# An encoder block in float32: output projection and second MLP product turned to tokens on partitions

## The chip, the cores and the metric

The kernel runs on one core of one Trainium2 chip. The metric is device microseconds from start to end of one execution, the median over runs. TensorE multiplies a stationary 128x128 operand with a moving one of up to 512 columns and writes PSUM, which has eight banks of [128, 512] float32. DVE, ScalarE (ACT in the profile) and GpSimd (POOL) do the elementwise work, and nearly all DMAs are issued by SyncE (SP). Each engine takes its instructions in the order in which the program lists them.

## The reference

One layer of an encoder block over x of [512 tokens, 2048 features], in float32. What matters here is its end:

```python
mix = (gate_a * y_a + gate_b * y_b) @ w_o[l] + b_o[l]
x = layer_norm(DEEPNORM_ALPHA * x + g1 * mix, ln1_g[l], ln1_b[l])
h = x * (1.0 + sc2) + sh2
f = jnp.square(jax.nn.relu(h @ w_m1[l] + b_m1[l])) @ w_m2[l] + b_m2[l]
x = layer_norm(DEEPNORM_ALPHA * x + g2 * f, ln2_g[l], ln2_b[l])
```

`w_o` is [2048, 2048], `w_m1` [2048, 8192], `w_m2` [8192, 2048]. Both norms go over the 2048 features of a token. `g1`, `sc2`, `sh2` and `g2` are vectors over the features, products of the conditioning vector with `w_ada`.

## The kernel before

**Products.** Each float32 operand is split into a high part of float32r's width and a low part (`split`, lines 74 to 77: a cast on ScalarE, a subtraction on DVE), and each product is three: high by high, high by low, low by high. Weights come in blocks of 256 rows and 512 columns (512 KB). `Weights` (lines 112 to 152) keeps three raw blocks in flight and three split ones ready. `take` hands out a block and, just before, splits the next and asks SP for the load of another, into the raw buffer that this split sets free.

**Where the work lies.** From the branches on, activations have features on partitions and tokens along the free side. `dense` (lines 157 to 205) makes four products of 128 output features by 512 tokens, or by half of the tokens (`tok`): weights are stationary, activations move. After each block of weights it runs the steps listed in `stages` for that block. These lists are written by hand, and they set the order of all other work on every engine.

**Projection and first norm (lines 960 to 978).** Column groups 0 and 1 of `w_o` are made for all tokens, groups 2 and 3 for the first half of the tokens and then for the second, so that the first half's norm runs beside the second half's products; their weights are loaded twice. `add_to` (line 905) empties four banks with one DVE step each (gate, line 902) and adds to the sums of the norm: squares on ScalarE, sums on POOL (line 826) and DVE (line 827). `Norm` (lines 799 to 872) works across partitions: it shifts by the first group's mean (lines 804 to 814), adds up over partitions with products of one column (line 848), and spreads the result over the partitions with other products (line 863).

**The MLP (lines 1013 to 1029)** goes in eight slabs of 1024 hidden features: two groups of `w1` (`hidden`, line 981), then four of `w2` in `add_to`. The first slab makes its `w1` groups by halves of the tokens, beside the late half's norm and input (`second_input`, line 930), and `skip_path` (line 993) scales the residual on POOL. All blocks of `w1` of that slab come twice.

**The last slab (lines 1031 to 1055)** makes `w2` groups 2 and 3 by halves; their split blocks stay in 16 tiles (`wkeep`), since they are used twice. The late half's last group is emptied bank by bank (`add_late`, line 910). Behind the last product come the sums, the root, their spreading and eighteen steps of `normal_2` (line 998) on DVE, POOL and ScalarE, with the output's DMAs.

Of the kernel before, what the change touches and what calls it, by code (L numbers as in the profile page):

```python
# [40 lines left out]
def block_kernel(ctx: ExitStack, tc: tile.TileContext, t):  # L41
# [38 lines left out]
    def blocks():  # L80
# [5 lines left out]
        def groups():  # L86
# [25 lines left out]
    class Weights:  # L112
        """Blocks of 256 rows and 512 columns: loaded three ahead of their split, split ahead of their use."""
# [15 lines left out]
        def tiles(self, what):  # L129
            """For the parts of a block; those of the last ones stay."""  # L130
            if what[0] == t["w_m2"].name and what[1] >= NSLAB * 4 - 2:
# [3 lines left out]
            return [wts.tile([P, 1024], F32R, name=n, tag=n) for n in ("whi", "wlo")]  # L135

        def prepare(self):
            while self.raw and len(self.ready) <= self.ahead:
# [6 lines left out]
        def take(self, w, cg, kp):  # L145
            if (w.name, cg, kp) in self.used:
                return self.kept[w.name, cg, kp]
            self.prepare()
# [8 lines left out]
    def dense_steps(out, w, cg, pairs, act, tok=ALL, by_token=False, stages=None, tail=None):  # L157
        """Four products of 512 columns of w: [features, tokens], or by_token [tokens, features].
        A step takes 256 rows; the last two, with tail, bank by bank, and tail follows each."""
# [3 lines left out]

        def products(i, kp, hi, lo):
            for j in range(2):
# [3 lines left out]
                if by_token:  # L169
                    s = slice(i * P, (i + 1) * P)  # L170
                    c = slice(512 * j, 512 * (j + 1))
                    terms = (ah[:, s], hi[:, c]), (ah[:, s], lo[:, c]), (al[:, s], hi[:, c])
                else:
                    s = slice(512 * j + i * P, 512 * j + (i + 1) * P)
                    terms = (hi[:, s], ah[:, tok]), (hi[:, s], al[:, tok]), (lo[:, s], ah[:, tok])
                for m, (a, b) in enumerate(terms):
                    nc.tensor.matmul(out[i], a, b, start=first and m == 0, stop=last and m == 2)  # L177
                if not tail or kp < pairs - 2:
                    yield

        kept = []
        for kp in range(pairs):
            hi, lo = weights.take(w, cg, kp)
            if tail and kp >= pairs - 2:
                kept.append((kp, hi, lo))
                if len(kept) == 2:
                    for i in range(4):
                        for k_ in kept:
                            for _ in products(i, *k_):
                                pass  # L190
                        tail(i, out[i])
            else:
                live = [products(i, kp, hi, lo) for i in range(4)]
                for _ in range(2):
                    for g in live:
                        next(g)
# [12 lines left out]
    def rstd_of(var):  # L209
        """[P, n] variances -> 1 / sqrt(max(var, 0) + eps), with a Newton step behind the table's root."""  # L210
# [27 lines left out]
    mean4 = const.tile([P, P], F32, name="mean4")  # L238
    nc.vector.memset(mean4, 1.0 / 512.0)

# [33 lines left out]
    spec = dram.tile([2, 2, 4, 2, P, 512], F32, name="spec")  # L274

# [3 lines left out]
    class Sine:  # L279
        """sin(freq * (product + bias)), its argument brought into the table's range."""  # L280
# [17 lines left out]
    def table(name, tiles):  # L298
        """cosines of the classes 0, 2, 1, 3, their sines, and -sines and -cosines of class 3."""
# [6 lines left out]
    class Forward:  # L306
        """Transform of four [128 tokens of a class, 512 channels] (classes 0..3), for angles below pi / 4
        and by symmetry the rest. Sums over the even positions, then with those over the odd."""
# [4 lines left out]
        def minus(self, out, a, b):  # L313
            """a - b of cosines; b - a of sines."""
# [13 lines left out]
        def odd(self):  # L328
            """Both sums over the odd positions, where the other kind's aren't wanted."""
# [15 lines left out]
    #: The spectra's parts: order, half of the channels, cosine or sine.  # L345
    PARTS = [(o, hf, cs) for o, hf in ((1, 1), (1, 0), (0, 0), (0, 1)) for cs in range(2)]

    class Filters:
        """The spectra: they go to DRAM but for the first to be used."""
# [15 lines left out]
        def fetch(self, n):  # L365
            """Last layer's weights and, in the row below, the skip's; with a half's first, its window."""
# [12 lines left out]
        def mixed(self, n):  # L379
            """Weights of the even and the odd parts of the taps."""  # L380
# [42 lines left out]
    def first_input(kc, xt):  # L423
        """x's chunk, modulated, in two parts."""
# [8 lines left out]
    def short_conv(ps, which, hf):  # L433
        """[128 channels, 512 tokens] x 4."""
# [93 lines left out]
    def to_tokens(src, cl, dst):  # L528
        """Four [128 channels, 512 tokens] -> [128 tokens of a class, 512 channels]."""
# [7 lines left out]
    class Conv:  # L537
        """A long convolution of four [128 tokens of a class, 512 channels], in stages."""
# [4 lines left out]
        def odd(self):  # L543
            """Sums over the classes 1 and 3, of cosines and sines, for both kinds of angles."""
# [35 lines left out]
        def fold(self, part):  # L580
            """Frequencies -> inputs of the inverse, by class of tokens, in three steps."""
# [21 lines left out]
    #: The column of a class in the tables.  # L603
# [11 lines left out]
    def inverse_T(conv, i, gate):  # L615
        """The same, [128 channels, 512 tokens], and its product's parts."""
# [18 lines left out]
    def into(conv, src):  # L635
        """Stages that lead from channels to the conv's two transforms."""
# [5 lines left out]
    def between(conv):  # L642
        """The same, in the next group."""
# [3 lines left out]
    def out_of(conv, gate, dst, after):  # L647
        """Stages that lead from a conv to the next one's first transform."""
# [147 lines left out]
    class Norm:  # L796
        """Sums of the deviations of [P, 512] chunks from the first group's mean, and of their squares."""

        def __init__(self):
# [348 lines left out]
```

## Time and profile before

| | us |
|---|---|
| median of 3 runs | 2803.61 (2803.1 to 2805.07) |
| profiled execution, its span from first to last instruction | 2800.5 |
| median less span: what lies around it | 3.1 |
| TensorE busy (97% of the span) | 2723.1 |
| DVE busy (54%) | 1509.0 |
| ScalarE busy (30%) | 830.8 |
| POOL busy (10%) | 274.6 |
| first product of `w_o` starts | 1157.60 |
| first product of `w2`, first slab, starts | 1445.17 |
| first product of `w2`, last slab, starts | 2663.76 |
| last product of `w2` ends, about | 2772.0 |

The profile is of one execution; it gives the span of that execution, and no other time of its own, so the 3.1 us compare it with the median. The starts in the lower part cut the span into stages. A busy TensorE is not one at its peak: products overlap, and their ends are modelled, so the pace is read from the distance between starts.

### The profile page before, as it was taken

To read this page: it belongs to the slowest core of one execution; us is meant where nothing else is said; L and a number is where in the kernel's file an instruction comes from. 1 tells how busy PE (TensorE), PEld (TensorE's weight loads), DVE (VectorE), ACT (ScalarE), POOL (GpSimd) and SP (SyncE) were. 2 spreads that over 40 slices of the span, in tenths; PEclk is the share of its full clock that TensorE was granted. 3 is DMA by queue.
4 is the path that set the end of the run, shared out by engine and by line. 5 is a ranking of instruction groups with operands and counts; after the bars stand their busy time and mean duration, and the time that the engine had idled before them with its cause. 6 is when DMAs were issued, how large, how long until landed. Compare 5 with 4: busy or idle time off the path is not lost.

```text
span 2800.5 us, 31575 instructions
## 1 busy us (share of the span) xinstructions
PE 2723.1 (97%) x12680; PEld 2243.0 (80%) x12680; DVE 1509.0 (54%) x1958; ACT 830.8 (30%) x1034; POOL 274.6 (10%) x222
## 2 busy tenths in 40 slices
PE   6899999999999999999999999999999999999986
PEld 2487777888888888889998888888888888888876
DVE  8976978554565556458863233433333334333276
ACT  3334223222223222434641222312222122221234
POOL 6510000000000000013740000000000000000034
PEclk9899999999999999999999999999999999999998
DMA  9673332555565567335553333332333333233322
GB/s 310 229 279 113 121 105 98 195 195 195 197 210 188 196 216 265 115 127 173 177 155 98 98 98 98 98 95 95 97 98 98 98 98 98 91 99 97 98 78 74
DMA packets 120020, 396.40 MB, mean 142 GB/s; under 512 B 13979, under 2 KB 18075, under 8 KB 119872
## 3 DMA queue, kind: packets, MB, share of 16 engines
q1 hardware_dynamic: 119872, 394.37, 43.0%
q8 instruction: 99, 1.62, 0.2%
q14 instruction: 49, 0.40, 0.0%
HBM read 383.84 MB, written 10.49 MB: 141 GB/s over the span
## 4 chain that ended last, share of the span: by engine, by line
PE 90%; DVE 5%; POOL 2%; issue 1%; DMA 1%; ACT 1%; SPq 0%; DVEq 0%; POOLq 0%; ACTq 0%
PE d L177 85%; DVE araw L264 1%; PE flt L393 1%; DVE xr L869 1%; POOL h L937 1%; DVE wlo L77 1%; DMA araw<-in_ada 1%; PE inv L621 1%; PE inv L609 0%; DVE ln_s L827 0%; PE f_o L334 0%; PE f_ee L322 0%; PE f_eo L326 0%; PE tr L532 0%; PE mix L743 0%
## 5 line engine op out<-in xcount | busy, mean ns | idle before, releaser
L177 PE MATMUL d<-act,whi 128*128 128x512 f32 (+1 forms) x5120 | 1456.7, 370 | 4.9 <-DVE bf_e L318 1.5
L77 DVE TENSOR_TENSOR wlo<-wraw,whi 128x1024 fp32r<-128x1024 f32 x488 | 602.2, 1237 | 1080.4 <-ACT whi L76 1077.2
L177 PEld LDWEIGHTS d<-act,whi 128*128 128x128 f32 x5120 | 927.5, 189 | 173.0 <-issue 7.7
L76 ACT CAST whi<-wraw 128x1024 fp32r<-128x1024 f32 x488 | 512.4, 1053 | 1498.3 <-PE d L177 1462.5
L177 PE MATMUL d<-act,wlo 128*128 128x512 f32 (+1 forms) x2560 | 943.4, 369 | 9.9 <-DVE wlo L77 9.9
L177 PEld LDWEIGHTS d<-act,wlo 128*128 128x128 f32 x2560 | 483.0, 189 | 92.2 <-DVE wlo L77 11.7
L177 PE MATMUL d<-fh,whi 128*128 128x512 f32 x960 | 373.9, 389 | 0.0
L177 PE MATMUL d<-fh,wlo 128*128 128x512 f32 x960 | 373.5, 389 | 0.0
L177 PE MATMUL d<-fl,whi 128*128 128x512 f32 x960 | 373.5, 389 | 0.0
L264 DVE SCALAR_TENSOR_TENSOR araw<-araw,cond 128x1024 f32<-128x1024 f32 x192 | 255.1, 1349 | 7.0 <-DMA araw<-in_ada 6.8
L824 POOL COPY ln_s<-xr 128x512 f32<-128x512 f32 x2 | 1.9, 936 | 2272.1 <-DVE xr L814 2272.1
L177 PEld LDWEIGHTS d<-fl,whi 128*128 128x128 f32 x960 | 180.2, 188 | 37.6 <-issue 0.2
L177 PEld LDWEIGHTS d<-fh,whi 128*128 128x128 f32 x960 | 180.2, 188 | 37.6 <-issue 0.2
L177 PEld LDWEIGHTS d<-fh,wlo 128*128 128x128 f32 x960 | 180.2, 188 | 37.4
L902 DVE SCALAR_TENSOR_TENSOR xr<-d,mod,xr 128x512 f32<-128x512 f32 (+1 forms) x160 | 102.6, 695 | 47.4 <-PE d L177 47.4
L177 PE MATMUL d<-whi,act 128*128 128x512 f32 x256 | 78.9, 389 | 0.0
L990 DVE TENSOR_TENSOR relu<-relu 128x512 f32<-128x512 f32 (+1 forms) x72 | 46.1, 640 | 38.5 <-ACT fh L989 38.4
L397 POOL TENSOR_TENSOR flt<-flt,win 128x512 f32<-128x512 f32 x32 | 62.8, 1987 | 5.2 <-ACT flt L395 4.8
L177 PE MATMUL d<-fh,wkeep 128*128 128x256 f32 x256 | 51.3, 300 | 10.0 <-DVE wkeep L77 10.0
L988 ACT ACTIVATE relu<-d,c_bm 128x512 f32<-128x512 f32 (+1 forms) x72 | 45.3, 629 | 38.5 <-PE d L177 38.5
L177 PEld LDWEIGHTS d<-whi,act 128*128 128x128 f32 x256 | 48.0, 188 | 9.9
L872 POOL TENSOR_TENSOR xr<-xr,ln_m 128x256 f32<-128x256 f32 x54 | 48.1, 902 | 54.0 <-DVE xr L869 54.0
(212 smaller groups left out, 1951.4 us busy)
## 6 DMA issues: line engine op xcount, KB each, us to landing
wraw<-in_w_m SPq DMA_DIRECT2D x272, 512.0 KB, 3.5
araw<-in_ada SPq DMA_DIRECT2D x192, 512.0 KB, 4.6
wraw<-in_w_in SPq DMA_DIRECT2D x144, 512.0 KB, 3.5
wraw<-in_w_o SPq DMA_DIRECT2D x48, 512.0 KB, 3.7
spec<-spec SPq DMA_DIRECT2D x48, 256.0 KB, 5.0
wraw<-in_w_b SPq DMA_DIRECT2D x16, 512.0 KB, 3.5
wraw<-in_w_a SPq DMA_DIRECT2D x16, 512.0 KB, 3.4
xT<-in_xT SPq DMA_DIRECT2D x16, 256.0 KB, 5.8
```

Source lines behind the costliest of these rows:

```text
L76: nc.scalar.copy(hi, src)
L77: nc.vector.tensor_tensor(lo, src, f32(hi), op=OP.subtract)
L177: nc.tensor.matmul(out[i], a, b, start=first and m == 0, stop=last and m == 2)
L264: nc.vector.scalar_tensor_tensor(raw, raw, 1.0, cond[:, 1024 * h:1024 * (h + 1)], op0=OP.mult, op1=OP.mult, accum_out=dots[:, m, kc, h:h + 1])
L393: nc.tensor.matmul(ps, self.a2[:k, cl, :], w[:k], start=True, stop=True)
L397: nc.gpsimd.tensor_tensor(x, x, win, op=OP.mult)
L621: nc.tensor.matmul(ps[:, cl * P:(cl + 1) * P], conv.y[cl][cs][:, s], ic(4 * cs + COLUMN[cl]), start=(cs == 0), stop=(cs == 1))
L869: nc.vector.tensor_tensor(x, x, self.rs[:, tok], op=OP.mult)
L872: eng.tensor_tensor(x, x, self.mr[:, tok], op=OP.add)
L902: nc.vector.scalar_tensor_tensor(x, ps, gate_[:, n:n + 1], x, op0=OP.mult, op1=OP.add)
L988: nc.scalar.activation(r, ps[i], AF.Relu, bias=bm1[:, n:n + 1], scale=1.0)
L990: nc.vector.tensor_tensor(r, r, r, op=OP.mult)
```

## The change

The output projection and the second MLP product are made with activations stationary and weights moving (`token_dense`), so that their results have 128 tokens on partitions and 512 features along the free side. The residual is loaded in that layout (a new input `x`, beside the transposed one), and the output leaves in it. Vectors over the features become rows, broadcast over the partitions: the two gates through a transpose, a store to DRAM and loads back (`gate_rows`), the others from a new input `rows`. Both norms take their moments with `bn_stats` along the free side; the class `Norm` is gone. The MLP's input goes back to features on partitions with transposes on TensorE (`turned`). In the first slab one group of `w1` is made by halves and the other for all tokens. In the last slab, column groups 2 and 3 are made for one tile of 128 tokens after the other, and each tile's norm and output follow it. `prepare` splits at most four blocks at a time and no longer counts the kept ones.

The diff, cut to its core (comments that go away, and functions that are only removed, are left out):

```diff
-                for cg in range(n) if s else (0, 1, 0, 1):
+                for cg in range(n) if s else (0, 0, 1):
...
         def prepare(self):
-            while self.raw and len(self.ready) <= self.ahead:
+            for _ in range(4):
+                if not self.raw:
+                    return
+                ring = sum(not self.keeps(r[2]) for r in self.ready)
+                if ring > self.ahead and not self.keeps(self.raw[0][1]):
+                    return
                 raw, what = self.raw.pop(0)
...
+    def gate_rows():
+        both = small.tile([P, 2, KC], F32, name="gcols", tag="gcols")
+        nc.scalar.copy(both[:, 0], mod[:, 2])
+        nc.scalar.copy(both[:, 1], mod[:, 5])
+        ps = bank("gT")
+        nc.tensor.transpose(ps[:2 * KC, :P], both.rearrange("p g k -> p (g k)"), ident)
+        rows_ = slot("gT")
+        nc.scalar.copy(rows_[:2 * KC, :P], ps[:2 * KC, :P])
+        for i in range(2):
+            nc.sync.dma_start(grow[i].rearrange("(k p) -> k p", p=P), rows_[i * KC:(i + 1) * KC, :P])
+    def row(src, name="row"):
+        return load(slot(name), src.broadcast_to([P, 512]))
+    gate_rows()
+    g1_row = [wts.tile([P, 1024], F32, name="g1row", tag="araw") for _ in range(2)]
+    for i, g in enumerate(g1_row):
+        load(g, grow[0:1, 1024 * i:1024 * (i + 1)].broadcast_to([P, 1024]))
+    load(cond, grow[1:2].broadcast_to([P, D]))
...
+    def residual(c):
+        gb = row(t["rows"][0:1, COLS[c]])
+        nc.gpsimd.tensor_scalar(gb, gb, 1.0 / ALPHA, None, op0=OP.mult)
+        nc.gpsimd.tensor_tensor(gb, gb, g1_row[c], op=OP.mult)
+        for i in TILES:
+            r[i][c] = load(slot("r"), t["x"][i][:, COLS[c]])
+            nc.gpsimd.tensor_tensor(r[i][c], r[i][c], gb, op=OP.add)
+    def token_dense(w, cg, pairs, act, tiles=TILES, stages=None):
+        out = {i: bank("t") for i in tiles}
+        for kp in range(pairs):
+            hi, lo = weights.take(w, cg, kp)
+            for j in range(2):
+                kc = 2 * kp + j
+                ah, al = act[kc]
+                c = slice(512 * j, 512 * (j + 1))
+                for i in tiles:
+                    s = slice(i * P, (i + 1) * P)
+                    for m, (a, b) in enumerate(((ah[:, s], hi[:, c]), (ah[:, s], lo[:, c]), (al[:, s], hi[:, c]))):
+                        nc.tensor.matmul(out[i], a, b, start=kc == 0 and m == 0, stop=kc == 2 * pairs - 1 and m == 2)
+            for f in (stages or {}).get(kp, ()):
+                f()
+        return out
+    def gated_1(ps, c, tiles=TILES):
+        for i in tiles:
+            x = slot("gated")
+            nc.vector.tensor_tensor(x, ps[i], g1_row[c], op=OP.mult)
+            nc.vector.scalar_tensor_tensor(r[i][c], r[i][c], ALPHA, x, op0=OP.mult, op1=OP.add)
+            nc.vector.bn_stats(st1[:, i, c], r[i][c])
+    def gated_2(ps, c, tiles=TILES, stats=False):
+        for i in tiles:
+            x = slot("gated")
+            nc.vector.tensor_tensor(x, ps[i], g2_row[c], op=OP.mult)
+            nc.vector.tensor_tensor(r[i][c], r[i][c], x, op=OP.add)
+            if stats:
+                nc.vector.bn_stats(st2[:, i, c], r[i][c])
...
+    def turned(tiles, kc, held):
+        ps, h = bank("h2T"), slot("h2")
+        for k in range(2):
+            s = slice((kc + k) % 4 * P, ((kc + k) % 4 + 1) * P)
+            for j, i in enumerate(tiles):
+                nc.tensor.transpose(ps[:, (2 * k + j) * P:(2 * k + j + 1) * P], r[i][kc // 4][:, s], ident)
+        for k in range(2):
+            s, n = slice(256 * k, 256 * (k + 1)), kc + k
+            nc.scalar.activation(h[:, s], ps[:, s], AF.Identity, bias=s2[:, n:n + 1], scale=a2[:, n:n + 1])
+        held.append(h)
...
+    def skip_path(c):
+        g, b, m = (row(t["rows"][k:k + 1, COLS[c]]) for k in (1, 2, 3))
+        nc.gpsimd.tensor_tensor(m, m, g2_row[c], op=OP.mult)
+        nc.vector.scalar_tensor_tensor(b, b, ALPHA, m, op0=OP.mult, op1=OP.add)
+        for i in TILES:
+            nc.vector.scalar_tensor_tensor(r[i][c], r[i][c], ALPHA, g, op0=OP.mult, op1=OP.mult)
+            nc.vector.tensor_tensor(r[i][c], r[i][c], b, op=OP.add)
...
+    residual(0)
+    gated_1(token_dense(w_o, 0, 8, mp, stages={2: [do(residual, 1)]}), 0)
+    gated_1(token_dense(w_o, 1, 8, mp, stages={2: [do(residual, 2)], 5: [do(residual, 3)]}), 1)
+    for tiles in (early, late):
+        for c in (2, 3):
+            stages = {}
+            if tiles is late and c == 2:
+                stages = norm_stages(early, 1)
+                for n in range(8):
+                    stages.setdefault(2 + n * 3 // 4, []).append(do(turned, early, 2 * n, held))
+            elif tiles is late:
+                stages = {1 + n: [do(second_input, early, 2 * n, held)] for n in range(7)}
+            gated_1(token_dense(w_o, c, 8, mp, tiles, stages), c, tiles)
...
+    def last_norm(i, spread):
+        mean, rstd = moments(st2, (i,))
+        shift = small.tile([P, 1], F32, name="shift", tag="shift")
+        nc.vector.scalar_tensor_tensor(shift, mean, -1.0, rstd, op0=OP.mult, op1=OP.mult)
+        for c in range(4):
+            x = r[i][c]
+            nc.scalar.activation(x, x, AF.Identity, bias=shift, scale=rstd)
+            nc.vector.tensor_tensor(x, x, ln2_g[c], op=OP.mult)
+            eng = nc.gpsimd if c in spread else nc.vector
+            eng.tensor_tensor(x, x, ln2_b[c], op=OP.add)
+            nc.sync.dma_start(t["out"][i][:, COLS[c]], x)
...
+            stages = merged({0: [do(second_input, early, KC - 2, held)]}, norm_stages(late, 0))
+            for n in range(8):
+                stages.setdefault(2 + n * 3 // 4, []).extend([do(turned, late, 2 * n, held), do(second_input, late, 2 * n, held)])
+            hidden(dense(w1, 0, 8, h2, tok_0, stages=stages), 0, f, tok_0)
+            hidden(dense(w1, 0, 8, h2, tok_1), 0, f, tok_1)
+            hidden(dense(w1, 1, 8, h2, stages={2 * c: [do(skip_path, c)] for c in range(4)}), 4, f)
...
+                gated_2(token_dense(w2, 4 * s + cg, SLAB // 2, f), cg)
...
+        gated_2(token_dense(w2, 4 * s, SLAB // 2, f), 0, stats=True)
+        ln2_g = [row(t["rows"][4:5, COLS[c]], "ln2") for c in range(4)]
...
+        gated_2(token_dense(w2, 4 * s + 1, SLAB // 2, f), 1, stats=True)
+        for i in TILES:
+            for c in (2, 3):
+                gated_2(token_dense(w2, 4 * s + c, SLAB // 2, f, (i,)), c, (i,), stats=True)
+            last_norm(i, (0, 2) if i < 3 else (1,))
```

`norm_stages` lists the moments of the tiles at its first stage and one column group's `normal_1` (a DVE step with mean and root) at each of four stages; `second_input` splits what `turned` made (a cast on ScalarE and a DVE step for each of two chunks); `moments` is an aggregation for each tile and the root of `rstd_of`. The gains and biases of the last norm (`ln2_g`, `ln2_b`) are loaded behind group 0 of the last slab.

## Rows read from the trace of the kernel before

**Rows 1.** busy time by stretch: us, PE, PEld, DVE, ACT, POOL, clock, DMA, GB/s

```profile
1157.60:1445.17 287.57, 278.06 (x1955) 260.80 (x1954) 202.57 (x279) 135.72 (x192) 120.48 (x104) 1.00 0.50 160
...
2663.76:2772.00 108.24, 97.90 (x595) 88.68 (x593) 79.25 (x103) 36.26 (x58) 44.53 (x39) 0.94 0.21 67
```

**Rows 2.** groups by shape, TensorE, 256 columns: xcount, busy us, mean ns, idle before

```profile
L177 PE MATMUL d<-act,whi 128*128 128x256 f32 x1024 | 185.2, 283 | 0.1
L177 PE MATMUL d<-act,wlo 128*128 128x256 f32 x512 | 145.6, 284 | 8.4 <-DVE wlo L77 8.4
...
L177 PE MATMUL d<-fh,wkeep 128*128 128x256 f32 x256 | 51.3, 300 | 10.0 <-DVE wkeep L77 10.0
...
L177 PE MATMUL d<-fl,wkeep 128*128 128x256 f32 x128 | 38.1, 297 | 0.0
```

**Rows 3.** timeline, TensorE: start us, us, what; every third product, wide and narrow

```profile
1600.01 0.39 PE L177 MATMUL d<-act,wlo 128*128 128x512 f32 x1
...
1600.69 0.39 PE L177 MATMUL d<-act,wlo 128*128 128x512 f32 x1
...
1284.98 0.28 PE L177 MATMUL d<-act,wlo 128*128 128x256 f32 x1
...
1285.34 0.28 PE L177 MATMUL d<-act,wlo 128*128 128x256 f32 x1
```

**Rows 4.** timeline, TensorE: eight transposes of an earlier stage

```profile
225.04 1.12 PE L532 MATMUL tr<-ident,hy 128*128 128x128 f32 x8
```

**Rows 5.** timeline, ScalarE: its last step ahead of the projection

```profile
1163.52 0.20 ACT L876 ACTIVATE warm<-inv_d 128x1 f32<-128x1 f32 x1
```

**Rows 6.** timeline, TensorE: behind the longest wait of the last slab

```profile
2726.46 0.80 PE L177 MATMUL d<-fh,wkeep 128*128 128x256 f32 x2 [6.44 <-DVE wkeep L77]
```

**Rows 7.** busy time by stretch, behind that wait

```profile
2728.00:2732.00 4.00, 4.00 (x21) 4.00 (x21) 3.98 (x3) 1.05 (x1) 1.75 (x1) 0.50 0.69 240
2732.00:2736.00 4.00, 4.00 (x33) 4.00 (x33) 2.19 (x6) 1.53 (x5) 1.41 (x2) 0.94 0.37 124
```

**Rows 8.** groups by shape, DVE: xcount, busy us, mean ns, idle before

```profile
L77 DVE TENSOR_TENSOR wlo<-wraw,whi 128x1024 fp32r<-128x1024 f32 x488 | 602.2, 1237 | 1080.4 <-ACT whi L76 1077.2
...
L902 DVE SCALAR_TENSOR_TENSOR xr<-d,mod,xr 128x512 f32<-128x512 f32 x128 | 89.2, 751 | 41.1 <-PE d L177 41.1
...
L827 DVE TENSOR_TENSOR ln_s<-ln_s,ln_sq 128x512 f32<-128x512 f32 x14 | 20.5, 1466 | 1.0
...
L787 DVE TENSOR_TENSOR sg<-sg,d 128x512 f32<-128x512 f32 x16 | 10.9, 682 | 0.3 <-PE d L177 0.3
...
L719 DVE BATCH_NORM_STATS2 st<-zv 128x6 f32<-128x512 f32 x8 | 4.9, 679 | 0.0
```

**Rows 9.** timeline, DVE and the DMA queue SP, in a slab of the MLP

```profile
1652.98 1.22 DVE L77 TENSOR_TENSOR wlo<-wraw,whi 128x1024 fp32r<-128x1024 f32 x1 [4.21 <-ACT whi L76]
...
1654.23 11.21 SPq L71 DMA_DIRECT2D wraw<-in_w_m  x3
```

**Rows 10.** DMA issues: xcount, KB each, median us from issue to landing

```profile
out<-out SPq DMA_DIRECT2D x16, 256.0 KB, 2.4
...
cond<-in_c SPq DMA_DIRECT2D x4, 256.0 KB, 4.0
...
sln<-in_sgu_lb SPq DMA_DIRECT2D x2, 256.0 KB, 7.4
```

**Rows 11.** timeline, DVE: behind the hidden group that ends at 1445.17

```profile
1448.63 1.23 DVE L77 TENSOR_TENSOR wlo<-wraw,whi 128x1024 fp32r<-128x1024 f32 x1
```

**Rows 12.** timeline, DVE: the last root, first and last step

```profile
2779.27 0.17 DVE L212 TENSOR_SCALAR rs<-ln_v 128x2 f32<-128x2 f32 x1
...
2780.70 0.16 DVE L854 SCALAR_TENSOR_TENSOR ln_m<-ln_m,rs 128x2 f32<-128x2 f32 x1
```

**Rows 13.** groups by shape, ScalarE: a pass with scale and bias

```profile
L898 ACT ACTIVATE xr<-xr,lnc 128x512 f32<-128x512 f32 x16 | 10.2, 712 | 0.0
```

**Rows 14.** groups by shape, POOL: a sum of 128x512

```profile
L826 POOL TENSOR_TENSOR ln_s<-ln_s,xr 128x512 f32<-128x512 f32 x14 | 21.4, 1526 | 28.7 <-DVE xr L902 27.7
```

More of the change, by code (lines that the diff above doesn't have):

```diff
@@ L147, in take @@
                 return self.kept[w.name, cg, kp]
-            self.prepare()
+            if not self.done or self.raw:
+                self.prepare()
             hi, lo, what = self.ready.pop(0)
@@ L168, in products @@
                 first, last = kc == 0, kc == 2 * pairs - 1
[L169 to L196, printed above, removed]
+                for i in range(4):
+                    if by_token:
+                        s = slice(i * P, (i + 1) * P)
+                        c = slice(512 * j, 512 * (j + 1))
+                        terms = (ah[:, s], hi[:, c]), (ah[:, s], lo[:, c]), (al[:, s], hi[:, c])
+                    else:
+                        s = slice(512 * j + i * P, 512 * j + (i + 1) * P)
+                        terms = (hi[:, s], ah[:, tok]), (hi[:, s], al[:, tok]), (lo[:, s], ah[:, tok])
+                    for m, (a, b) in enumerate(terms):
+                        nc.tensor.matmul(out[i], a, b, start=first and m == 0, stop=last and m == 2)
             for f in (stages or {}).get(kp, ()):
@@ L884, in block_kernel @@
+    lnc = const.tile([P, 2, KC], F32, name="lnc")
+    a2, s2 = (lnc[:, i] for i in range(2))
+    sc2, sh2 = mod[:, 4], mod[:, 3]
     nc.vector.tensor_mul(a2, ln1_g, sc2)
@@ L943, in normal_both @@
-    def normal_both(k, tok):
-        if k < 2:
-            normal_1(k, tok)
-        else:
-            second_input(k - 2, tok, k if k < KC else None)
-    def spread_over(step, tok, first, k0=0, k1=KC, n=2):
-        return {first + i // n: [do(step, k0 + j, tok) for j in range(i, min(i + n, k1 - k0))]
-                for i in range(0, min(k1 - k0, n * (8 - first)), n)}
-    def prepare(cg, k):
-        return {k: [do(residual, 4 * cg + i) for i in range(4)],
-                k + 1: [do(ln1.shifted, r1[4 * cg + i]) for i in range(4)] if cg else []}
+    TILES = range(4)
@@ new lines, in row @@
+    def row(src, name="row"):
[5 more added lines that the diff above has]
+    load(cond, grow[1:2].broadcast_to([P, D]))
+    g1_row = [g1_row[c // 2][:, c % 2 * 512:(c % 2 + 1) * 512] for c in range(4)]
+    g2_row = [cond[:, s] for s in COLS]
+    r = [[None] * 4 for _ in TILES]
@@ new lines, in moments, with normal_1 @@
+    def moments(st, tiles):
+        m = small.tile([P, len(tiles), 2], F32, name="moments", tag="moments")
+        for k, i in enumerate(tiles):
+            nc.vector.bn_aggr(m[:, k], st[:, i])
+        return m[:, :, 0], rstd_of(m[:, :, 1])
+    h2 = []
+    def normal_1(mom, tiles, c):
+        for k, i in enumerate(tiles):
+            nc.vector.tensor_scalar(r[i][c], r[i][c], mom[0][0][:, k:k + 1], mom[0][1][:, k:k + 1],
+                                    op0=OP.subtract, op1=OP.mult)
@@ new lines, in second_input @@
+    def second_input(tiles, kc, held):
+        tok, h = slice(tiles[0] * P, (tiles[-1] + 1) * P), held.pop(0)
+        for k in range(2):
+            if kc + k == len(h2):
+                h2.append(act_pair(kc + k))
+            hi, lo = (x[:, tok] for x in h2[kc + k])
+            split(h[:, 256 * k:256 * (k + 1)], hi, lo)
+    def skip_path(c):
[5 more added lines that the diff above has]
+            nc.vector.tensor_tensor(r[i][c], r[i][c], b, op=OP.add)
@@ new lines, in norm_stages @@
+    def norm_stages(tiles, first):
+        out = {first: [lambda: mom[tiles].append(moments(st1, tiles)), do(normal_1, mom[tiles], tiles, 0)]}
+        for k in range(1, 4):
+            out.setdefault(first + k, []).append(do(normal_1, mom[tiles], tiles, k))
+        return out
+    residual(0)
[3 more added lines that the diff above has]
+        for c in (2, 3):
+            stages = {}
+            if tiles is late and c == 2:
[5 more added lines that the diff above has]
+            gated_1(token_dense(w_o, c, 8, mp, tiles, stages), c, tiles)
@@ L1054, in block_kernel @@
-        for k in range(KC + 2):
-            normal_2(k, late)
+        gated_2(token_dense(w2, 4 * s, SLAB // 2, f), 0, stats=True)
+        ln2_g = [row(t["rows"][4:5, COLS[c]], "ln2") for c in range(4)]
+        ln2_b = [wts.tile([P, 1024], F32, name="ln2b", tag="araw") for _ in range(2)]
+        for i, g in enumerate(ln2_b):
+            load(g, t["rows"][5:6, 1024 * i:1024 * (i + 1)].broadcast_to([P, 1024]))
+        ln2_b = [ln2_b[c // 2][:, c % 2 * 512:(c % 2 + 1) * 512] for c in range(4)]
```

210 lines of the change are left out of this document (26 added, 184 removed).

## The prediction

> **What bounds the kernel now.** I read the table of busy time by stretch first. The change touches the stretch from the first output-projection product to the first second-MLP product (287.57 us), and the last slab: 108.24 us to its last product and 28.5 us more to the end of the span at 2800.5 [rows 1]. TensorE is busy through nearly all of the first two, so its own work is the first term. The groups by shape come next: of the products that stream 256 columns, 1024 + 512 are in the projection and the first slab, 256 + 128 in the last one, and their idle column holds the waits, 8.4 us for the weights' low part and 10.0 us for the kept one [rows 2]. The timeline gives the pace: three wide products (512 columns) in 0.68 us, 0.227 each; three narrow ones in 0.36 us, 0.12 each [rows 3]. So a narrow one costs 53% of a wide one, not 50%. The seven slabs in between take 1218.6 us from start to start, which is 7 x 768 wide products and nothing else; they stay as long. The program took a median of 2803.61 us in the runs, 3.1 over the profiled span; I make the sum against the span and add it to the median, holding the 3.1 as it is.
>
> **TensorE's own work.** Projection and first slab hold now 384 wide and 1536 narrow products: 87.0 + 184.3 = 271.4 us. Afterwards the projection is 768 wide (174.1), the first slab's first MLP product 384 narrow and 192 wide (46.1 + 43.5): 263.7, **-7.7**. What 287.6 holds over 271.4, **16.2** us, is the 8.4 of waits and the small products of the norm over partitions with their waits; all that goes. New are 64 transposes of 128x128 for the MLP's input. Eight such took 1.12 us [rows 4]: **+9.0**.
>
> **The gate rows.** They need a product of their own ahead of the projection, in TensorE's queue. Its input is two ACT copies behind the square root's table load and the warm-up, which ended at 1163.72 [rows 5]. Now the projection starts at 1157.60 without asking for that. Two copies at 0.2, product and start: about 1164.4, so 6.8 us idle. What idling costs afterwards: behind a wait of 6.44 us [rows 6] the granted clock stood at 0.50, the lower level, from 2726.46 to about 2732.4 [rows 7]; half of that is lost, 2.8. **+9.6.** The DMAs to DRAM and back (0.5 + 0.5 + 1 MB) and the residual's are in front of weight loads on SP, but two split and three raw blocks, 27 us of products, stand ready.
>
> **Emptying the banks.** A 128x512 tile takes three DVE steps now, with rows to price them [rows 8]: product with the gate 0.68, sum 0.75, statistics 0.68, about 2.05 with overlap; four tiles 8.2. DVE starts them some 1.8 before a group's end, since the first bank is full nine products early. Then the next low part, 1.24, is ready 7.6 after the start of the group. In a full group the third block is wanted at 10.9: covered. In the half groups a block is 12 wide products, 2.72, and the third is wanted at 5.44. So the group behind column group 1 waits 2.2, and 0.5 more for POOL beside it. Half groups empty two tiles (4.1): 5.3, just in time. In the late half the first transposes wait for emptying, moments and the first normalized chunk: 1.3. In the first slab's two half passes DVE and ACT carry the late norm, its transposed input and the split as well; followed instruction by instruction the third and fourth blocks come 1.6 late in one pass and 3.6 in the other. With one fall of the clock (1): **+10**. In the slabs between, four tiles cost 5.4 (two steps) and the low part is ready at 6.6 of 10.9: nothing.
>
> **The skip path.** It stood on POOL, off everyone's way. Now it is four steps on DVE in the second column group of the first slab, one every two blocks, and its three rows are asked for when it begins. SP is behind the weights' loads, each of which waits for the low part before: a load was issued 0.03 us after such a step ended [rows 9]. So nothing is fetched early. From the end of a low part: a weight load and three rows, 0.44 each to issue, the last one's issue 1.3 behind. Rows of 256 KB spread over the partitions landed 4.0 after their issue (the conditioning vector) and 7.4 (gains of an earlier norm) [rows 10]. I take 5.8, about the middle, since these queue behind the weights' 512 KB: 7.1. Then POOL's product, 1.4 (1.53 beside DVE), then DVE: one step 0.75 and eight of 0.68 to 0.75, overlapped in pairs (5.5). D = 14.9 us in which DVE waits or works and no low part can pass. Two low parts more make 17.4 for two blocks that take TensorE 10.9. The first low part of the group is done 4.7 after it starts, as it was behind the same emptying at 1448.63 + 1.23 [rows 11]. The second MLP product's second low part is then at 4.7 + 4 x 14.9 + 7 x 1.24 = 73; emptying the hidden group and one more low part are 6.7, so its third block starts at 79.7 in place of 54.4: **+25**.
>
> **The last slab.** TensorE has 4 x 96 wide products, 87 us, and none of today's 10.0 us of waits. DVE sets the end. Time 0 is the end of column group 0 (21.8 in). DVE empties it until 6.4, then makes ten low parts. Three raw buffers hold them back: a load starts only after the low part three before, so the last is done at 26 (wanted at 31). Emptying group 1: 34.2. Each token tile costs DVE 4.1 for two tiles, moments and root 1.8 (1.6 today between the first and the last of those steps [rows 12], and the aggregation), 0.8 for ScalarE's first pass (0.71 [rows 13]), 4.0 for six of the eight steps with gain and bias, the other two on POOL, and 1.5 for POOL beside DVE: 12.2 against TensorE's 10.9. Three tiles: 70.8. The last: 4.1 + 1.8 + 0.8 + 4.6 + 0.8, 82.9, and 3.6 for issue and landing of the output (landing 2.4 [rows 10], and what the span holds around it): 86.5. Altogether 21.8 + 86.5 = 108.3 in place of 136.7: **-28.4**. The 1.5 is from the row in which a DVE sum took 1.47 beside POOL's 1.53 and not the 0.68 of the step next to it [rows 8, 14]: nearly 0.8 for each of two. The Trainium skill (SBUF — State Buffer, "Who interferes with whom") says that a DVE instruction with two SBUF inputs and a GpSimd instruction that reads SBUF exclude each other for a whole instruction. By that rule the two would cost 3.0 a tile, which speaks against handing POOL two sums; no row here shows the full block.
>
> **The sum.** -7.7 - 16.2 + 9.0 + 9.6 + 10 + 25 - 28.4 = +1.3: 2804.9 us, **2805**. About 0.2%, 5.6 us, is what a measurement of this kernel can tell from no change. The gain at the end is given back in the middle.
>
> **The rivals.** (1) The rows come sooner. At 4.0 from issue to landing D is 13.1, the loss 18: 2798. For it: no other stream of loads runs there but the weights. Against: four loads at once. (2) The end is shorter: if POOL's two sums cost DVE nothing and the kept blocks land in 3.5 without queueing behind the 2 MB of rows, DVE is done some 7.5 earlier: 2797. (3) Slower: the row loads of the skip path, in the second column group of the first slab, take what the gains took, 7.4 from issue. Then D is 16.5, the loss 31: 2811. It decides from D = 16.0 on. For it: those were broadcast rows, as these are; against: the modulations' loads ran beside those. (4) POOL and DVE exclude each other fully: 3 x 1.5 + 0.7 more at the end, 2810. (5) The change doesn't do what it says, the tile-by-tile end: this is inside my sum, for TensorE's order of tiles sets nothing where DVE is 1.3 us a tile behind; were TensorE to wait for kept blocks as it does now, 10 more. I hold that below one in twenty, in (3)'s share.
>
> **How the numbers follow.** Forecast 0.36; (1) 0.18 and (2) 0.16, together faster 0.34; (3) 0.24 and (4) 0.06, together slower 0.30. The forecast's own range is 2799 to 2809. For the 8 in 10 I let D go from 12 to 17 (loss 14 to 33), the last slab from -36 to -22 and the other stalls by 4 either way; not all at one end: 2786 to 2823.
>
> **What would show it.** Right: TensorE idle for 6 to 7 us before the projection's first product, at half clock behind it; four waits for the weights' low part in the second group of the first slab, DVE's idle time there ended by POOL's product and that by the rows' DMA; no wait for kept blocks; the last product about 20 us before the end, DVE busy without a break behind it. Wrong: if the skip path's rows are landed before DVE asks for them, the loss of 25 falls away and the kernel is faster by some 24; if TensorE still waits in the last slab, it is slower by that wait.

## The result: 0.2% slower, two large errors that nearly cancel

The kernel after the change takes 2808.42 us (median of 19 runs, 2805.22 to 2812.62), the kernel before in the same session 2803.16 (19 runs, 2801.89 to 2805.07): ratio 1.0019, interval [1.0012, 1.0025], 5.3 us slower. The forecast was 2805, in the class "within 0.2%", with the range 2786 to 2823; 5.3 is just inside the 5.6 us that the prediction set for that class.

The profiled execution took 2811.11 us, 1.8 over its span of 2809.3. It lies 2.7 above its median. Every run here lists a time 1.8 over its span, so the profiled execution of the kernel before, of 2800.5 us, took about 2802.3, 0.9 below its median; the 3.1 that the prediction added to the span held that scatter too. So the two spans differ by 8.8 where the medians differ by 5.3. The part of the program that the change leaves alone holds 2.2 of the 8.8: its last product starts at 1159.56 instead of 1157.37. It starts late, by 1.0 to 2.2 us, in all seven traces of kernels with the change; with one trace of the kernel before, how much of that is scatter stays open.

The page of the kernel after, its span and its busy times:

```profile
span 2809.3 us, 29794 instructions
...
PE 2719.5 (97%) x11909; PEld 2204.5 (78%) x11909; DVE 1537.2 (55%) x2032; ACT 788.8 (28%) x965; POOL 149.7 (5%) x99
```

But for POOL's, these shares hardly differ from before (97, 54, 30 and 10%), and tell nothing of what happened. The table of busy time by stretch does, cut where the work changes: projection and first `w1` group, second `w1` group, the four `w2` groups of the first slab, and the last slab's `w2` groups (us, PE, PEld, DVE, ACT, POOL, clock, DMA, GB/s):

```profile
1166.20:1403.73 237.53, 233.59 (x1218) 200.16 (x1218) 135.61 (x189) 95.47 (x142) 35.66 (x24) 0.98 0.51 171
1403.73:1471.76 68.03, 50.49 (x194) 40.25 (x193) 28.84 (x42) 12.49 (x18) 3.89 (x3) 0.85 0.42 105
1471.76:1567.93 96.17, 90.24 (x386) 74.13 (x385) 49.08 (x61) 19.90 (x22) 1.30 (x1) 0.96 0.29 96
2699.45:2786.50 87.05, 87.04 (x384) 71.72 (x383) 64.87 (x99) 24.02 (x30) 6.74 (x4) 1.00 0.34 115
```

By the pace of [rows 3] the second line holds 43.5 us of products and the third 87.0; they took 68.0 and 96.0. (The cuts at 1567.93 and 2699.45 lie 0.16 us behind the starts of the next stages' first products, at 1567.77 and 2699.29; the sums below go by these starts, so the 33.6 us of the first expectation are 33.5 here.) The first holds 220.2 of products (174.1 + 46.1) and took 237.5. The fourth takes exactly its 87.0 at full clock: no wait is left there. What TensorE waited for, summed from 1150 us to the end (us, times, longest):

```profile
PE d L187 <- DVE wlo L77: 18.3, 4, 6.9
PE t L849 <- DVE wlo L77: 8.4, 2, 5.9
PE gT L807 <- ACT gcols L805: 6.2, 1, 6.2
PE h2T L889 <- DVE r L880: 0.5, 2, 0.3
```

The waits for `wkeep` [rows 2] are gone. New are the one for ScalarE ahead of the gate rows and four long ones for the low part. The spans' difference by stage, against the forecast's terms:

| term | forecast | measured |
|---|---|---|
| products, old waits and small products | -23.9 | -23.9 (the base of the next two rows) |
| gate rows, clock, transposes, emptying | +28.6 | +23.7 (6.4 idle, 17.3 over the products) |
| skip path | +25 | +33.5 (68.0 - 43.5, and 96.0 - 87.0) |
| last slab, start of its `w2` to the end | -28.4 | -26.7 (110.0 for 136.7) |
| the part ahead, unchanged | 0 | +2.2 |
| sum | +1.3 | +8.8 |

The skip path is the largest loss, and its place can be read line by line. The kernel after, timeline of DVE, SP, POOL and TensorE in the second `w1` group (start, us, what, and in brackets the idle time before it with what ended it):

```profile
1407.19 1.23 DVE L77 TENSOR_TENSOR wlo<-wraw,whi 128x1024 fp32r<-128x1024 f32 x1
...
1408.82 1.37 SPq L71 DMA_DIRECT2D row<-in_rows  x3
...
1417.31 1.29 POOL L907 TENSOR_TENSOR row<-row,cond 128x512 f32<-128x512 f32 x1 [160.11 <-DMA row<-in_rows]
...
1418.64 0.69 DVE L908 SCALAR_TENSOR_TENSOR row<-row 128x512 f32<-128x512 f32 x1 [10.22 <-POOL row L907]
...
1423.96 0.69 DVE L911 TENSOR_TENSOR r<-r,row 128x512 f32<-128x512 f32 x1
1424.57 2.35 DVE L77 TENSOR_TENSOR wlo<-wraw,whi 128x1024 fp32r<-128x1024 f32 x2
...
1425.84 0.80 PE L187 MATMUL d<-act,wlo 128*128 128x512 f32 x1 [5.15 <-DVE wlo L77]
1445.08 0.79 PE L187 MATMUL d<-act,wlo 128*128 128x512 f32 x1 [5.50 <-DVE wlo L77]
1464.71 0.79 PE L187 MATMUL d<-act,wlo 128*128 128x512 f32 x1 [6.89 <-DVE wlo L77]
1483.52 0.79 PE L849 MATMUL t<-wlo,fh 128*128 128x512 f32 x1 [5.93 <-DVE wlo L77]
```

DVE ends a low part at 1408.42. Only then SP asks for three rows; POOL's product starts when they have landed, at 1417.31; DVE stands still until 1418.64 and works until 1424.65. Between the two low parts lie 16.2 us, in which TensorE has two blocks, 10.9 us, to work on. The low part that comes next sits behind the waiting step in DVE's queue, though its block is loaded. It happens four times: DVE's wait for POOL's row, in the view that sums waits (us, times, longest), and the landing of all sixteen rows, the four of the residual among them (least, median, most):

```profile
DVE row L908 <- POOL row L907: 43.1, 4, 11.3
```

```profile
DMA to landing us min/median/max: 5.3/7.4/8.1
```

Behind the fourth wait TensorE runs at its lower level for nearly 6 us more (the clock is the third number from the right):

```profile
1483.52:1487.50 3.98, 3.98 (x9) 3.14 (x10) 3.88 (x7) 0.00 (x0) 0.00 (x0) 0.50 0.43 132
1487.50:1491.50 4.00, 4.00 (x15) 3.19 (x14) 3.52 (x4) 0.00 (x0) 0.00 (x0) 0.77 0.12 17
```

The end of the kernel after: aggregations of the four token tiles on DVE, and inside the first tile one of the sums that POOL takes beside DVE's own:

```profile
2759.17 0.27 DVE L873 BATCH_NORM_AGGREGATE moments<-st 128x2 f32<-128x24 f32 x1
...
2762.73 1.72 POOL L962 TENSOR_TENSOR r<-r,ln2b 128x512 f32<-128x512 f32 x1 [1286.44 <-DVE r L960]
...
2763.34 1.66 DVE L962 TENSOR_TENSOR r<-r,ln2b 128x512 f32<-128x512 f32 x1
...
2772.04 0.26 DVE L873 BATCH_NORM_AGGREGATE moments<-st 128x2 f32<-128x24 f32 x1
...
2784.93 0.26 DVE L873 BATCH_NORM_AGGREGATE moments<-st 128x2 f32<-128x24 f32 x1
...
2797.80 0.26 DVE L873 BATCH_NORM_AGGREGATE moments<-st 128x2 f32<-128x24 f32 x1
...
2805.51 0.69 DVE L962 TENSOR_TENSOR r<-r,ln2b 128x512 f32<-128x512 f32 x1
```

The distance of the aggregations is 12.87, 12.89 and 12.87 us: each tile costs DVE 12.9, TensorE only 10.9, so DVE sets the end.

### The profile page after: what moved, and what is told of

Same layout as the page of the kernel before. It is cut to its first block, busy times and chain, and to the rows that moved or that the text cites. A ratio compares the mean times of both kernels' runs of the same rounds, so it can differ in the third digit from the quotient of the medians.

```text
span 2809.3 us, 29794 instructions
## 1 busy us (share of the span) xinstructions
PE 2719.5 (97%) x11909; PEld 2204.5 (78%) x11909; DVE 1537.2 (55%) x2032; ACT 788.8 (28%) x965; POOL 149.7 (5%) x99
## 4 chain that ended last, share of the span: by engine, by line
PE 84%; DVE 5%; DMA 3%; ACT 1%; issue 1%; SPq 0%; POOL 0%; DVEq 0%; ACTq 0%; POOLq 0%
PE d L187 54%; PE t L849 28%; DMA row<-in_rows 1%; DVE wlo L77 1%; DMA xT<-in_xT 1%; PE inv L611 1%; PE inv L599 0%; DMA wraw<-in_w_m 0%; ACT whi L76 0%; DVE r L960 0%; DVE r L962 0%; DVE r L910 0%; DVE r L865 0%; SPq L71 0%; DVE r L911 0%
## 5 line engine op out<-in xcount | busy, mean ns | idle before, releaser
L187 PE MATMUL d<-act,whi 128*128 128x512 f32 (+1 forms) x4224 | 1283.0, 386 | 3.9 <-DVE bf_e L308 1.5
L187 PEld LDWEIGHTS d<-act,whi 128*128 128x128 f32 x4224 | 786.5, 189 | 167.8 <-issue 7.2
L187 PE MATMUL d<-act,wlo 128*128 128x512 f32 (+1 forms) x2112 | 812.5, 385 | 20.4 <-DVE wlo L77 20.4
L849 PE MATMUL t<-wlo,fh 128*128 128x512 f32 x960 | 374.8, 390 | 5.9 <-DVE wlo L77 5.9
L849 PE MATMUL t<-whi,fl 128*128 128x512 f32 x960 | 374.5, 390 | 0.0
L849 PE MATMUL t<-whi,fh 128*128 128x512 f32 x960 | 374.4, 390 | 0.0
L849 PEld LDWEIGHTS t<-wlo,fh 128*128 128x128 f32 x960 | 180.8, 188 | 43.9 <-DVE wlo L77 6.4
L849 PEld LDWEIGHTS t<-whi,fl 128*128 128x128 f32 x960 | 180.9, 188 | 37.7
L849 PEld LDWEIGHTS t<-whi,fh 128*128 128x128 f32 x960 | 180.8, 188 | 37.7
L849 PE MATMUL t<-whi,act 128*128 128x512 f32 x512 | 162.5, 397 | 0.0
```

Of the source, the lines that this page charges most:

```text
L849: nc.tensor.matmul(out[i], a, b, start=kc == 0 and m == 0, stop=kc == 2 * pairs - 1 and m == 2)
```

## The experiments

The theory: the loss sits in three places, the rows asked for too late in the skip path, the gate rows ahead of the projection, and POOL's sums beside DVE's at the end; and the last slab could be shorter if DVE had the kept blocks done earlier. Rivals: the skip path loses by DVE's eight steps for each column group and not by the wait; POOL's help shortens the end. All times are medians beside runs of the kernel before on the same chip (2803.67 over 21 runs for the first four kernels, 2803.52 over 9 for the last two); these and the 2803.16 above agree within 0.5 us, so the kernels are compared with the 2808.42 of the kernel after directly.

**Rows of the skip path asked for two blocks earlier.**

```diff
+    skip_row = {}
...
+    def skip_rows(c):
+        skip_row[c] = [row(t["rows"][k:k + 1, COLS[c]]) for k in (1, 2, 3)]
     def skip_path(c):
-        g, b, m = (row(t["rows"][k:k + 1, COLS[c]]) for k in (1, 2, 3))
+        g, b, m = skip_row.pop(c)
...
-            hidden(dense(w1, 0, 8, h2, tok_1), 0, f, tok_1)
-            hidden(dense(w1, 1, 8, h2, stages={2 * c: [do(skip_path, c)] for c in range(4)}), 4, f)
+            hidden(dense(w1, 0, 8, h2, tok_1, stages={4: [do(skip_rows, 0)]}), 0, f, tok_1)
+            hidden(dense(w1, 1, 8, h2, stages={2 * c: [do(skip_path, c)] + ([do(skip_rows, c + 1)] if c < 3 else [])
+                                               for c in range(4)}), 4, f)
```

> The three rows of each step of the skip path are asked for two blocks (or half a group) before the step; nothing else changes. Theory (the loss of 33.6 us in the second group of the first slab is DVE standing still for the rows' loads): DVE's wait ahead of each step falls from 10.2 to 11.2 us to about 1.5 (POOL's product), a step takes 8 us in place of 17, two blocks cost DVE 10.4 of the 10.9 us that TensorE needs, and the four waits of TensorE for the low part go. 30 to 34 us less than the changed kernel, about 2776. Rival (DVE's eight sums for each step are the load, whenever they come): less than 8 us gained, the waits for the low part stay at 3 us or more each.

Measured: 2776.34 us (4 runs, 2774.38 to 2779.99), ratio 0.9903 [0.9889, 0.9916]: 32.1 below the kernel after, and 27 below the one before. From 1400 to 1490 us no TensorE instruction waits any more, and in its timeline the first of the four steps follows the low part at once:

```profile
1407.79 1.22 DVE L77 TENSOR_TENSOR wlo<-wraw,whi 128x1024 fp32r<-128x1024 f32 x1
1408.92 0.69 DVE L913 SCALAR_TENSOR_TENSOR row<-row 128x512 f32<-128x512 f32 x1
...
1414.23 0.69 DVE L916 TENSOR_TENSOR r<-r,row 128x512 f32<-128x512 f32 x1
1414.84 2.35 DVE L77 TENSOR_TENSOR wlo<-wraw,whi 128x1024 fp32r<-128x1024 f32 x2
...
1419.25 0.69 DVE L913 SCALAR_TENSOR_TENSOR row<-row 128x512 f32<-128x512 f32 x1 [2.05 <-POOL row L912]
```

DVE does the same nine steps; between two low parts now lie 5.9 us (1409.01 to 1414.92), and 8.1 where POOL's row still comes 2.05 late. With the two low parts, 2.35, that is 8.3 and 10.4 of the 10.9 that TensorE has for two blocks, so it fits and nothing is lost. The wait was what made it a loss.

**The eight steps left out, the wait kept.** This kernel leaves out the scaling of the residual by gain and its sum with the bias, so it computes something else; it stands for what the steps alone cost.

```diff
         nc.vector.scalar_tensor_tensor(b, b, ALPHA, m, op0=OP.mult, op1=OP.add)
-        for i in TILES:
-            nc.vector.scalar_tensor_tensor(r[i][c], r[i][c], ALPHA, g, op0=OP.mult, op1=OP.mult)
-            nc.vector.tensor_tensor(r[i][c], r[i][c], b, op=OP.add)
```

> Of the skip path the eight sums and products with the residual are left out (the residual is not scaled, so the output is another); rows, POOL's product and the one DVE step that waits for it stay where they are. Theory: the wait of 10 to 11 us ahead of each step stays, D falls from 17 to 12, so the four waits of TensorE shrink but don't go: 18 to 22 us less than the changed kernel, about 2788. Rival (the sums are the load): all waits go, 32 us less.

Measured: 2787.95 us (4 runs, 2786.19 to 2790.69), ratio 0.9944 [0.993, 0.9957], 20.5 below the kernel after. The two gains, 32.1 and 20.5, are not shares of the 33.5. Each is measured against the limit of 10.9 us for two blocks: wait and steps make 16.8 + 2.3 = 19.1, the steps alone 8.3 and fit, the wait alone some 14 and does not fit. DVE still waits for POOL's row as long as before, and TensorE still waits for the low part, though less. (Of the six waits summed here two, of 3.08 and 0.76, come ahead of the skip path; its own four are 2.58, 3.11, 1.00 and 0.70, for 23.5 in all in the kernel after.)

```profile
PE d L187 <- DVE wlo L77: 6.5, 3, 3.1
PE gT L807 <- ACT gcols L805: 6.2, 1, 6.2
PE t L849 <- DVE wlo L77: 4.8, 3, 3.1
...
DVE row L908 <- POOL row L907: 43.0, 4, 11.4
```

So the rival (the steps are the load, whenever the rows come) is ruled out: without the wait they cost nothing, and only on top of it do they cost 20.5.

**The gate rows inside the first projection group.** They are made behind the second block of weights, with the residual's first column group; the second follows at the fifth block.

```diff
-    gate_rows()
...
-    load(cond, grow[1:2].broadcast_to([P, D]))
...
+    def gates():
+        gate_rows()
...
+        load(cond, grow[1:2].broadcast_to([P, D]))
...
-    residual(0)
-    gated_1(token_dense(w_o, 0, 8, mp, stages={2: [do(residual, 1)]}), 0)
+    gated_1(token_dense(w_o, 0, 8, mp, stages={1: [gates, do(residual, 0)], 4: [do(residual, 1)]}), 0)
```

> The gates' transpose, their store and loads and the first residual move behind the second block of the projection's first group. Theory (TensorE stood behind a product that waits for ScalarE, and then ran at half clock): the 6.2 us of wait and 2 to 3 us of the lower clock go, 8 to 9 us less than the changed kernel, about 2800. Rival (the wait moves on: the first gate rows are now late, and DVE, emptying the first group, waits for the gates or the residual): under 3 us gained, and a wait of DVE for a DMA or for POOL at the end of the first group.

Measured: 2800.84 us (11 runs, 2798.47 to 2804.6), ratio 0.999 [0.9981, 0.9999], 7.6 below the kernel after, somewhat short of what was expected. In the kernel after, the wait and the stretch behind it stand as follows, first in the timeline, then by stretch:

```profile
1166.15 0.40 PE L807 MATMUL gT<-ident,gcols 128*32 128x128 f32 x1 [6.21 <-ACT gcols L805]
1166.20 0.78 PE L849 MATMUL t<-whi,act 128*128 128x512 f32 x1
```

```profile
1168.00:1172.00 4.00, 4.00 (x11) 3.07 (x10) 1.04 (x1) 0.00 (x0) 0.00 (x0) 0.51 0.63 215
1172.00:1176.00 4.00, 4.00 (x19) 3.29 (x18) 0.25 (x1) 1.05 (x1) 0.00 (x0) 1.00 1.00 381
```

and in the timeline of this one, where the same product waits for nothing, and by stretch:

```profile
1170.40 0.27 PE L807 MATMUL gT<-ident,gcols 128*32 128x128 f32 x1
```

```profile
1168.00:1172.00 4.00, 4.00 (x20) 3.22 (x19) 1.77 (x3) 1.21 (x2) 0.00 (x0) 1.00 0.58 163
```

The clock stays at 1.00 where it had been 0.51. So the idle time and the fall of the clock behind it were both the price of that one wait. The rival is out: up to the end of the second column group DVE waits for no DMA and for no row of POOL.

**No sums of the last norm on POOL.**

```diff
-            last_norm(i, (0, 2) if i < 3 else (1,))
+            last_norm(i, ())
```

> In the last norm all sums with the bias are on DVE, none on POOL. Theory (a DVE sum and a POOL sum exclude each other: the DVE sum beside POOL took 1.64 to 1.67 us and not 0.69): a tile costs DVE 12.3 in place of 12.9 us, the end comes 2 us sooner. Rival (as the prediction had it, POOL takes two of eight sums off DVE at half their price): the end comes no sooner or up to 2 us later.

Measured: 2806.23 us (11 runs, 2804.58 to 2811.28), ratio 1.0009 [1.0, 1.0018], 2.2 below the kernel after. Against scatter this is at the edge of what the runs can tell; the distance of the aggregations is clear:

```profile
2756.62 0.26 DVE L873 BATCH_NORM_AGGREGATE moments<-st 128x2 f32<-128x24 f32 x1
2760.09 0.69 DVE L962 TENSOR_TENSOR r<-r,ln2b 128x512 f32<-128x512 f32 x1
...
2768.91 0.26 DVE L873 BATCH_NORM_AGGREGATE moments<-st 128x2 f32<-128x24 f32 x1
```

A tile takes DVE 12.3 instead of 12.9 although it has two sums more to do. POOL's help costs more than it saves. From the first aggregation to the end of the span, the four traces with POOL's sums take 50.1 us each, the three without 48.2: 1.9 of the 2.2. The whole last slab is hardly shorter in this one trace (109.9 for 110.0), since DVE waited 9.2 us for the casts of kept blocks and not 7.4; these waits come to 7.4 to 9.2 us in the six traces that make the kept blocks behind group 0.

**The three together.**

> The skip path's rows early, the gates inside the first group and the last norm's sums on DVE, all three together. Theory (three separate losses): the gains add up, 32.1 + 7.6 + 2.2 = 41.9 us less than the changed kernel, about 2766.5. Rival (they share a resource, DVE or the DMA queue, so that one gain uncovers another wait): less than 36 us together, 2772 or more.

Measured: 2766.78 us (4 runs, 2765.82 to 2767.95), ratio 0.9869 [0.9855, 0.9882]. The three gains against the kernel after, 32.1, 7.6 and 2.2, add up to 41.9, and 2808.42 - 41.9 = 2766.5. They lie in three stages and, as far as the medians can tell, don't touch one another.

**The three, and the kept blocks split earlier.** With those gone, the end of the kernel is again DVE's: it makes all kept low parts behind group 0. Here `prepare` makes one kept block beside each block of groups 0 and 1.

```diff
-                for cg in (0, 1, 2, 3):
+                for cg in (0, 1, 2, 3) if s < NSLAB - 1 else ():
                     yield w2, s * 4 + cg
...
+        n = SLAB // 2
+        for k in range(2 * n):
+            yield w2, (NSLAB - 1) * 4 + k // n, k % n
+            yield w2, (NSLAB - 1) * 4 + 2 + k // n, k % n
...
-                self.ready.append((hi, lo, what))
+                if not self.keeps(what):
+                    self.ready.append((hi, lo, what))
...
-            if (w.name, cg, kp) in self.used:
+            if self.keeps((w.name, cg, kp)):
+                while (w.name, cg, kp) not in self.kept:
+                    self.prepare()
```

> The same, and in the last slab the eight blocks that are kept are loaded and split in between the blocks of column groups 0 and 1, not behind them. Theory (DVE's chain of work sets the end: today it waits 7.4 us for kept blocks' casts, which wait for loads held back by three raw buffers, and only then empties group 1): the last kept split is done before TensorE ends group 1, emptying starts 6 to 7 us sooner, and the end moves by as much: about 2760. Rival (TensorE's order of tiles or the output's DMAs set the end): no gain, 2766.

Measured: 2761.46 us (5 runs, 2759.63 to 2763.55), ratio 0.9847 [0.9834, 0.9861], 5.3 below the one before it and 42 below the kernel before the change. It is the fastest kernel here. The gain falls about 1 us short, and the timeline shows where DVE now waits for TensorE:

```profile
2693.09 1.22 DVE L77 TENSOR_TENSOR wkeep<-wraw,wkeep 128x1024 fp32r<-128x1024 f32 x1 [3.00 <-ACT wkeep L76]
2698.52 0.69 DVE L875 TENSOR_TENSOR gated<-t,cond 128x512 f32<-128x512 f32 x1 [4.20 <-PE t L860]
2711.44 0.69 DVE L875 TENSOR_TENSOR gated<-t,cond 128x512 f32<-128x512 f32 x1 [2.60 <-PE t L860]
```

The kept blocks are done before group 1 ends, and DVE stands idle for 4.2 and 2.6 us. Emptying of group 1 starts about 7 us sooner, counted from the slab's first product, and 2.6 of that are lost again at the first tile's second bank: from there TensorE's order sets the start of the first token tiles, DVE the rest.

## Why the prediction was right, and where it was not

**The place of each loss was right.** TensorE stood idle for 6.4 us ahead of the projection (6.8 forecast) with the clock at 0.51 behind it; four waits for the low part came with the skip path, three in the second `w1` group and one just behind it; DVE's own waits ahead of them were ended by POOL's product, and POOL's by the rows; no wait for kept blocks was left, and DVE was busy up to the end. The class, within 0.2%, holds. That is luck in part: terms were off by +8.5, -4.9 and +1.7, as the table shows, so the closeness says little for the sizes, more for the places.

**The skip path was mis-sized: 25 forecast, 33.5 measured.** The step that failed is the choice of 5.8 us from issue to landing, "about the middle" between 4.0 and 7.4 [rows 10]. The rows came at 7.4 (median), and the last of each three, for which POOL waits, 7.4, 8.1, 7.7 and 7.7 after its issue: the end that rival (3) had priced, or beyond; its D of 16.5 and loss of 31 are nearer than the forecast's 14.9 and 25. The four D measure 16.2, 17.0, 17.4 and 16.5, 67.1 in all for the 59.6 forecast: +7.5. The first low part was done 4.7 after the group's start, as forecast, and seven others took 8.0 us for the 8.7 forecast: -0.7. So the second low part of the `w2` group was there at 79.7, not at 73. Behind it I had let DVE's emptying set the third block, 6.7 later. In fact TensorE's second block did, most of it at half clock: its last 23 products took 8.1, from 1483.52 to 1491.61. That is +1.4 that the working lacked, and the third block started at 87.9 in place of 79.7. The first kernel of the experiments shows the other half of the statement: with the rows there in time, 32.1 of the 33.5 go away ("faster by some 24" was forecast, and is short by the same error).

**Emptying, transposes and clock were over-sized: 28.6 forecast, 23.7 measured.** The wait behind column group 1 was 2.44 for the forecast 2.2 + 0.5. But the two half passes, followed "instruction by instruction" to 1.6 and 3.6 of lateness, gave one wait of 0.76 for the low part, and the transposes waited 0.5 in place of 1.3. That is the term that failed: the 10 came to some 5.3, 3.7 of waits and, by the 0.60 behind the wait of 2.44, about 1.6 of lower clock. Why DVE and ACT kept up there was not tried. Half the clock behind the gates' wait, 2.8 forecast, fits [rows 7] and the 0.51; with about 2.9 for it, 9.1 of the 17.3 are left for the transposes, 9.0 forecast.

**The last slab was right to 1.7 us.** 110.0 for 108.3. The kept low parts were done at 2746.86, within 1 us of the forecast; each tile cost 12.9 and not 12.2. The step is "1.5 for POOL beside DVE", by the row of 1.47 [rows 8]. With POOL at work a DVE sum takes 1.63 to 1.67, not 1.47 (two of them 1.9 more than alone, not 1.5), and POOL's sum, 1.3 alone, takes 1.6 to 1.8. The other 0.2 of a tile lie in emptying and moments. The Trainium skill (SBUF — State Buffer, "Who interferes with whom") says that a DVE instruction with two SBUF inputs and a GpSimd instruction that reads SBUF exclude one another for a whole instruction. The trace agrees: DVE's sum that began at 2763.34 beside POOL's of 2762.73 ended at 2765.00, 0.55 after POOL's end at 2764.45: less than the 0.69 that it takes alone, so most of it ran when POOL had ended. So rival (4)'s mechanism was there: its full price was 3 x 1.5 + 0.7 = 5.2 above the forecast, and the end came 1.7 above it. The run without POOL shows what it costs: 2.2 us, where DVE with two sums more is faster by 0.6 a tile.

**The shift of the unchanged part, 2.2, was no term.** The profiled execution lies 2.7 above its median, but the part ahead is late by 1.0 or more in the other traces too; what shifts it is not shown.

**The rivals.** (1), rows sooner, did not happen: no row landed in less than 5.3. (2), a shorter end, did not either. (3) happened: D lay above the 16.0 at which it decides, and the loss was 33.5 for its 31. The lighter half passes gave 4.9 back, and 2808.42 lies between the forecast and its 2811. (5) is out: the tile-by-tile end does what it says, as no TensorE wait is left from 2699.29 on.

## What to carry to other kernels

A wait placed on a queue holds up everything behind it, so a step whose inputs come from a DMA belongs behind the issue of that DMA by its measured landing time (7.4 us here), not beside it: asking two blocks earlier gave 32 us for a dozen lines of order. Compare, for each stretch, the holding engine's time with what the bound engine has ready (8.3, 14 and 19.1 of 10.9 us): the loss is what lies above that, and gains of single repairs do not add up within it. Helping a busy engine with another can cost more than it saves where the two hold each other up: two sums of 0.69 us moved to POOL made a tile 0.6 us longer.

## What the runs showed of the hardware that was not expected

Three waits of TensorE of nearly equal length were followed by different clocks. Behind 2.44 us in the kernel after (1264.29) the granted clock was 0.60 in the next 4 us; behind 2.58 us in the kernel without the eight steps it stayed at 1.00; behind 3.11 us in the same kernel it was 0.65. In the timeline and by stretch, the kernel after, then the other:

```profile
1264.29 0.80 PE L849 MATMUL t<-wlo,act 128*128 128x512 f32 x1 [2.44 <-DVE wlo L77]
...
1264.30:1268.30 4.00, 4.00 (x11) 3.22 (x12) 2.21 (x2) 0.00 (x0) 0.00 (x0) 0.60 0.64 193
```

```profile
1436.06 0.50 PE L187 MATMUL d<-act,wlo 128*128 128x512 f32 x1 [2.58 <-DVE wlo L77]
...
1436.10:1440.10 4.00, 4.00 (x18) 3.27 (x19) 1.04 (x1) 0.00 (x0) 0.00 (x0) 1.00 0.69 211
1450.40:1454.40 4.00, 4.00 (x12) 3.17 (x13) 1.07 (x1) 0.00 (x0) 0.00 (x0) 0.65 0.68 194
```

So a wait of this length costs its own time and, in two of three places, about 1.5 us more (4 us at 0.60 or 0.65 lose 1.6 or 1.4). The wait behind column group 1, the first of the three, stands in all seven traces of kernels with the change. It was 2.18, 2.19, 2.23, 2.44, 2.47, 3.08 and 3.11 us long, and the clock over the next 4 us was 1.00, 1.00, 0.59, 0.60, 0.67, 0.50 and 0.58. Each time it cost either nothing more or, as an estimate from these clocks, 1.3 to 2.0 us; what decides it stays open.

The row loads of 256 KB that are spread over the partitions landed in 5.3 to 8.1 us, the weights' 512 KB in 3.5 (median, the page of the same kernel): a load of half the size took about twice as long. That the spreading is the cause is not shown: the residual's tiles, 256 KB that are not spread, landed in 6.1 (median), and the rows are asked for in threes right behind weight loads; asked for earlier, in the first experiment, they landed in 4.2 to 8.1.
